# The RWKV inverse of a two-layer diffusion block: its broadcast load and its store laid out 32 by 4 instead of 4 by 32

## The chip, the core and the metric

The kernel runs on one core of a Trainium2 chip. A core has a matrix engine (TensorE, PE in the rows, with its weight loads as PEld), three engines for elementwise work (VectorE DVE, ScalarE ACT, GpSimd POOL), a queue engine that issues transfers (SyncE, SP) and 16 DMA engines that carry them out. Each engine works through its own list of instructions in order, and waits on semaphores for what others write. The metric is the device time of one execution in microseconds (us), lower is better; the figure compared is the median over runs.

## What is computed

Two layers over 512 latent tokens (x) and 256 context tokens (z) of width 1024. Each layer normalises, multiplies by one wide input projection, and feeds three token mixers: gated linear attention, windowed attention and a bidirectional RWKV-7 mixer. The mixers' outputs are merged, projected and added, and a gated feed-forward part follows. The RWKV mixer is, for each direction, a recurrence over tokens:

```
def step(S, inp):
    w_t, k_t, v_t, kk_t, a_t = inp[:5]
    sa = jnp.einsum('bhvk,bhk->bhv', S, kk_t)
    S = S * w_t[:, :, None, :] - sa[..., None] * (kk_t * a_t)[:, :, None, :] + v_t[..., None] * k_t[:, :, None, :]
    return S, jnp.einsum('bhvk,bhk->bhv', S, inp[5])
```

## The kernel before

The recurrence is done in chunks of 32 tokens. Within a chunk the dependence of each token on the earlier ones is a unit triangular 32 by 32 matrix, and the chunk needs its inverse. Four chunks (128 tokens, a "half" in the code) and 8 heads make 32 such blocks, which `inverse` (from line 1508) inverts together. There are 12 halves a layer, 6 in each direction, so 24 calls in all. The forward ones ("f") do their arithmetic on VectorE, the backward ones ("b") on GpSimd.

One call goes through these steps. All of its transfers are issued from SP.

- `prep` (from line 1450) loads `cp`, `bk` and `kr` (lines 1459 to 1461) and makes the scores `X`.
- Line 1516 stores the two quadrants of `X` to a DRAM tile `d1` (two DMAs of 64 KB).
- Line 1518 loads `d1` back, blocks on partitions, four copies of each block: `L`, 128 partitions of 4 KB, 512 KB.
- Line 1521 loads a start value (four pieces of a unit matrix) into `G`, 128 KB. `G` and `L` have two buffers each, shared by both directions, so this load can start only when an earlier half's `G` has been stored.
- Lines 1532 and 1533 run 31 pairs of multiply (`ftmp`) and subtract on `G` and `L`.
- Line 1536 stores `G` to a second DRAM tile `d2`, 128 KB in runs of 128 bytes, and line 1538 loads it back as `TT`, turned so that the matrix engine can use it.

A block's four partitions share its 32 rows: each works on the rows of one residue mod 4. `chain` (from line 1541) then takes the chunks of a half one after the other: `yp` (product with the state), `ysb` (ACT), `up` (product with `TT`, line 1584), `uv` (copies by DVE and ACT, line 1593), `sp` (line 50), `sblk` (the new state, DVE). `run` moves two such lanes, forward and backward, in turn. `ahead` lets the front (`prep` and `inverse`) of a lane run one half ahead in layer 0 and two in layer 1.

Beside these lanes the matrix engine works on products that need no mixer (`px`, `pz`), whose weights come as `raw` (512 KB each, line 66) and are split into `wh` (ACT, line 71) and `wl` (DVE, line 72). `paced` ties these products to the lanes' progress.

The order on each engine, SP's included, is not the order of the code. The kernel is built with a scheduler that simulates it with its own estimates of durations and sets each engine's order from that. A change in the code therefore reorders instructions far from it. Transfers complete when all their pieces have landed; SP itself issues in order, so a transfer that waits for data holds back all those behind it. The names in the rows leave buffer numbers out: `d` is both DRAM tiles, so `L<-d` is the load of line 1518, `d<-G` the store of line 1536 and `TT<-d` the load of line 1538.

Of the kernel before, what the change touches and what calls it, by code (L numbers as in the profile page):

```python
# [9 lines left out]
F32 = mybir.dt.float32  # L10
# [10 lines left out]
KD = 8  # L21
# [3 lines left out]
FREE, PER = 150, 3.3  # see paced()  # L25
# [3 lines left out]
class Kern:  # L29
# [18 lines left out]
    # ---------------------------------------------------------------- helpers  # L48
# [8 lines left out]
    def after(self, i, j):  # L57
        """instruction i, not before j in their engine's program"""
        self.tc.add_manual_dep(i.ins, j.ins.name, mybir.DependencyInfo(mybir.DependencyClass.NoSync, mybir.DependencyReason.DATA), reason="order")
        return i  # L60

    def wunit(self, src, n):
        """the next weights, split: per 128 columns the high and the low parts"""
# [20 lines left out]
    def hop(self, i):  # L84
        """a product of a chain that others are paced by"""
        if self.hops is not None:
            self.hops.append(i)

    def paced(self, i, ps):
        """beside a chain: the first FREE products (of 512 columns) as they come, then at most PER more after each one of the chain,  # L90
        so that those of the chain never queue behind many others"""
        if self.hops is not None:
            if self.done >= FREE and self.hops:
                self.after(i, self.hops[min(int((self.done - FREE) / PER), len(self.hops) - 1)])
            self.done += ps.shape[-1] / 512

    def room(self, n):
        """whether n more products fit the pace"""
        return self.done + n <= FREE + PER * len(self.hops)
# [10 lines left out]
    def run_job(self, later=None):  # L110
        """the next queued job; what a job returns is its second half, left to the caller if `later` is a list"""
# [14 lines left out]
    def rsqrt(self, y, s, t):  # L126
        """y = s ** -0.5 (s, y, t: same-shape SBUF tiles)"""
# [7 lines left out]
    def rsqrt_v(self, y, s, t):  # L135
        """y = s ** -0.5 without table functions: a guess from the halved exponent, three Newton steps"""
# [9 lines left out]
    # ---------------------------------------------------------------- consts  # L146
# [32 lines left out]
    # ---------------------------------------------------------------- adaLN  # L179
    def ada(self, l, bank, R, rbufs):  # L180
        """generator: modulation vectors of layer l, one round per 2048 columns; bank(shape, name): a PSUM tile, R: pool of the weights"""
# [36 lines left out]
    # ---------------------------------------------------------------- norm  # L218
    def stats(self, xk, a, b, P, tags, S, y):
        """generator: y <- 1 / rms of the tokens a..b-1 (rows 32 j: j-th quarter); P, tags: PSUM pool and (tag, bufs) of its one-bank tiles;  # L220
        S: pool of temporaries"""
# [18 lines left out]
    def spread(self, y, n, P, tags, S):  # L240
        """the n values of y, over all partitions (PSUM)"""
# [9 lines left out]
    def norm(self, xk, a, b, P, tags, S, apply):  # L251
        """generator: rmsnorm of the tokens a..b-1; apply(k, r): emits what follows for the k-th feature tile, r: 1 / rms over all partitions"""
# [10 lines left out]
    # ---------------------------------------------------------------- mixer input  # L263
    def gemm_x(self, w):
        """one 128-column tile of the input projection of the x tokens, feature-major"""
# [15 lines left out]
    def new_h(self, Z=None):  # L281
        """tiles of the two parts of h; Z: pool of the z tokens, where they lie apart"""
# [3 lines left out]
    def h(self, j, k, a, b):  # L286
        """part j (high, low) of the tokens a..b-1 of h, k-th feature tile"""
        return self.hz[j][k][:, a - NX:b - NX] if self.hz and a >= NX else self.hs[j][k][:, a:b]

    def norm_mod(self, xk, a, b, A, sh, P, tags, S, y=None):  # L290
        """generator: h = rmsnorm(x) * g * (1 + scale) + shift of the tokens a..b-1, split into two float32r parts;
        y: the tokens' 1 / rms, where they are known"""
# [21 lines left out]
    # ---------------------------------------------------------------- layers  # L314
    @contextmanager
    def weights(self, name, bufs, side=None):
        """pool of the weight tiles of the jobs to come; raw ones of their own only at the outermost level"""
# [14 lines left out]
    def fill(self):  # L332
        """one queued job, if any"""
# [6 lines left out]
    def mixed(self, gen, steps, spread):  # L340
        """run the mixer `gen` (about `steps` steps) with the queued jobs spread over it"""
# [9 lines left out]
    def layer(self, l, X, xs):  # L351
# [76 lines left out]
        with self.pool(f"pf{l}", space=PSUM) as pg:  # L428
# [5 lines left out]
            # layer 1: paced by the chain; layer 0, where TensorE is the bound: evenly from the start  # L434
# [30 lines left out]
        # merge, output projection, feed-forward  # L465
# [30 lines left out]
    def branch_jobs(self, l, n):  # L496
        """gated output projections of the first two mixers, summed into accd"""
# [24 lines left out]
    # tokens in two groups: those whose third mixer output comes last (0..127, 384..511) and the others  # L522
# [8 lines left out]
    def branch_operand(self, l, late, raw):  # L531
        """the third mixer's output of one group of tokens, in two parts"""
# [6 lines left out]
    def branch_gemm(self, l, w, m, late, g):  # L539
        """g <- gated product of one group of tokens"""  # L540
# [6 lines left out]
    def last_branch(self, l, n, P):  # L547
        """the third mixer's projection of the first group, added to what accd holds: the first group's operand of the output projection"""
# [18 lines left out]
    def gemm_parts(self, w, nk, rh, rl, parts):  # L567
        """products of the tokens of each part: (PSUM, first token, end)"""
# [51 lines left out]
    def two_parts(self, xs, parts, update, norm, keep=6):  # L620
        """the last KD queued jobs for the first part of the tokens, then for the second, with the first part's norm beside them;
        returns the second part's norm, not yet finished"""
# [25 lines left out]
    def ffn(self, l, n, xs):  # L648
# [3 lines left out]
        with self.ps, self.pool(f"fA{l}") as A:  # L652
# [27 lines left out]
            # the last update in two parts of the tokens, each part's norm as soon as it is there  # L680
# [19 lines left out]
            # the first tiles while the second part's norm is finished  # L700
# [22 lines left out]
    def final(self, xs, a, b, N, S):  # L723
        """generator: the final norm of the tokens a..b-1"""
# [30 lines left out]
# ------------------------------------------------------------------ gated linear attention  # L755
class Gla:
    """one layer's bidirectional gated linear attention; chunks of 128 tokens: x 0..3, z 4..5"""
# [77 lines left out]
    def cum(self, hp):  # L835
        """per-chunk cumulative log gates (times 16) of both directions for head pair hp"""
# [21 lines left out]
    def states(self, hp, B):  # L858
        """scaled queries, and the state before every chunk, of both directions"""
# [164 lines left out]
# ------------------------------------------------------------------ windowed attention  # L1024
class Swa:
    """one layer's grouped-query attention; tile t holds heads t and t + 4, key-value head g the rows 64 g"""

    def __init__(self, K, l, P, ps, yb):
# [13 lines left out]
        # float32r parts: a head's queries as (high; low) in one order of the row halves, keys twice  # L1042
# [5 lines left out]
    def add_jobs(self, P):  # L1048
        """projection jobs; P: pool of what only they need"""
# [46 lines left out]
    def run(self, T):  # L1096
# [4 lines left out]
        # the softmax of one group of heads beside the value products of the group before  # L1101
# [13 lines left out]
    def values(self, T, n, g, keys, r):  # L1115
        """generator: transposes of the weights, value products of one group of heads; its output when both groups are there"""
# [99 lines left out]
# ------------------------------------------------------------------ RWKV-7  # L1216
class Rwkv:
    """one layer's RWKV-7 mixer; tokens: x 0..511, z 512..767; halves of 128 tokens: x 0..3, z 4..5"""
# [9 lines left out]
    def open_f(self):  # L1228
        """what the projection jobs need"""
# [15 lines left out]
        self.hb = P.tile([128, 16], F32, name="hb")  # half of w0 (f p0..3, b p0..3), a0  # L1245
# [43 lines left out]
    # -- evacuation of a projected tile with the centred shift mix  # L1289
# [10 lines left out]
    def add_jobs(self, J, ps, psn):  # L1300
        """projection jobs; J: pool of temporaries, ps/psn: PSUM pool and (tag, bufs) of its one-bank tiles"""
# [14 lines left out]
        def lowrank(half, di, p, t):  # L1316
            """tanh of half the low-rank product plus half the offset"""
# [36 lines left out]
        def keys(p):  # L1354
            """normalised keys, and the two directions' replacement vectors and keys, of head pair p"""
# [67 lines left out]
    def knorm(self, J, bank, big, kt):  # L1423
        """1 / max(|k * k_k|, 1e-12) per head: rows 32 (token block) + head, columns x 0..127, z 128..191"""
# [23 lines left out]
    # -- decays and scores of 128 tokens of one direction  # L1448
    def prep(self, d, g):
# [31 lines left out]
        # transposed scores, rows (even chunk: B~ j, k~ j; odd chunk: k~ j, B~ j), columns (K~ i, r~ i)  # L1481
# [26 lines left out]
    def inverse(self, d, g):  # L1508
        """T = (I + L)^-1 of 32 blocks (4 chunks x 8 heads), four partitions per block (row mod 4)"""
        nc, T = self.nc, self.T  # L1510
        d1 = self.D.tile([2, 16, 32, 32], F32, name="d1", tag="d1", bufs=3)   # q, (e w p), j, i
        d2 = self.D.tile([8, 4, 32, 32], F32, name="d2", tag="d2", bufs=3)    # (q e w), p, j, i
# [5 lines left out]
        nc.sync.dma_start(L.rearrange("u j i -> u (j i)"), d1.rearrange("q u j i -> (q u) (j i)").unsqueeze(0).to_broadcast([4, 32, 1024]))  # L1518
# [17 lines left out]
        nc.sync.dma_start(d2.rearrange("m p (a s) i -> s (m p) a i", s=4), G)  # L1536
# [4 lines left out]
    def chain(self, it):  # L1541
        """generator: the chunks of one half of one direction"""
# [73 lines left out]
    def tail(self, g, y):  # L1616
        """group norm, bonus and gate of 128 tokens -> yc; rows of y: 32 (head pair) + token, columns: chunk, head, value"""
# [44 lines left out]
    def run(self):  # L1662
        """generator over the mixer's steps; yields "fill" where other work may be emitted"""
# [119 lines left out]
def _layout(x, c, ctx, c_ctx, w_ada, b_ada, g_mix, g_ffn, w_in, w_gk2, b_gk, g_gla, sink, mu_shift, w0, w_w2, a0, w_a2,  # L1783
            w_g2, k_k, k_a, r_k, gn_w, gn_b, w_branch, w_out, w_ffn1, w_ffn3, w_ffn2, g_final):
    f = np.float32
    D = {}
# [74 lines left out]
```

## Time and profile before

| what | value |
|---|---|
| time, three runs | 3356.23, 3366.86 and 3367.24 us, median 3366.86 |
| span of the profiled execution | 3361.6 us |
| PE busy over the span | 3033.8 us (90%) |
| DVE, ACT, POOL busy | 1756.6, 1081.2 and 990.4 us (52%, 32%, 29%) |
| mean granted clock of TensorE | 0.921 |
| DMA engines, the main queue | 34.2% of 16 engines' span |
| `L<-d`, `d<-G`, `TT<-d`, `G<-gid` | 24 each |

The span is the time from the first to the last instruction of one profiled execution. The profile gives no other time for that execution, so what lies around the span isn't shown; the median of the runs is 5.3 us above it. The granted clock is the share of full speed that TensorE was allowed: 1.00 is its upper level (2.4 GHz), 0.50 its lower one (1.2 GHz). The mixer's inverses lie in two stretches, about 645 to 1100 us (layer 0) and 2390 to 2870 us (layer 1).

### The profile page before, as it was taken

Reading aid. Unit: us, or ns where it says so; the run is one execution under the profiler, and the core shown is the slowest. Engines: PE = TensorE matmul, PEld = TensorE weight load, DVE = VectorE, ACT = ScalarE, POOL = GpSimd, SP = SyncE. Lnnn points to the kernel's source line nnn. Section 1 sums busy time; section 2 is a strip of 40 time slices with the busy share of each in tenths; the row PEclk is TensorE's granted clock in tenths of the full one; section 3 lists DMA queues with packets and bytes.
Section 4 is the critical chain, followed back from the end, with each engine's and each line's share of the span. In section 5 each row is a group of like instructions: output and inputs, shape, how many; then the busy total and the mean of one; then the engine's idle time right before and its main releaser. Section 6 shows DMA issues by size and latency. Waiting matters only on the chain. (4 is left out here: it accounts for less than half of the span.)

```text
span 3361.6 us, 62705 instructions
## 1 busy us (share of the span) xinstructions
PE 3033.8 (90%) x25760; PEld 2400.0 (71%) x25760; DVE 1756.6 (52%) x3506; ACT 1081.2 (32%) x2034; POOL 990.4 (29%) x1438
## 2 busy tenths in 40 slices
PE   6999999878889989999999899698857789799998
PEld 3777877666666778888888787576635466788887
DVE  3175557766656755222223454656567566643335
ACT  3255444422222233212122344453322222332223
POOL 2033122344655322101001211312266465221102
PEclk9999999888888999999999899798868679899999
DMA  7421222544345552443212322123633444512223
GB/s 289 153 74 56 96 101 95 174 131 124 99 119 142 168 197 73 153 157 132 63 63 95 96 73 95 58 76 126 205 103 107 112 131 137 187 69 95 96 98 119
DMA packets 269375, 398.33 MB, mean 118 GB/s; under 512 B 94624, under 2 KB 179360, under 8 KB 269088
## 3 DMA queue, kind: packets, MB, share of 16 engines
q1 hardware_dynamic: 249184, 370.20, 34.2%
q10 hardware_dynamic: 19904, 24.12, 2.0%
q8 instruction: 202, 3.31, 0.4%
q14 instruction: 85, 0.70, 0.1%
HBM read 320.33 MB, written 73.92 MB: 117 GB/s over the span
## 5 line engine op out<-in xcount | busy, mean ns | idle before, releaser
L50 PE MATMUL px<-hh,wl 128*128 128x512 f32 x1584 | 646.5, 408 | 31.9 <-DVE wl L72 31.8
L50 PE MATMUL px<-hh,wh 128*128 128x512 f32 x1584 | 651.9, 412 | 14.1 <-ACT wh L71 6.5
L50 PE MATMUL px<-hl,wh 128*128 128x512 f32 x1584 | 643.2, 406 | 11.6 <-POOL hl L302 8.8
L72 DVE TENSOR_TENSOR wl<-raw,wh 128x1024 fp32r<-128x1024 f32 (+1 forms) x314 | 402.3, 1282 | 366.4 <-ACT wh L71 332.1
L71 ACT ACTIVATE wh<-raw 128x1024 fp32r<-128x1024 f32 (+1 forms) x314 | 326.1, 1041 | 778.8 <-PE pz L50 395.2
L50 PEld LDWEIGHTS px<-hh,wl 128*128 128x128 f32 x1584 | 308.2, 195 | 110.0 <-DVE wl L72 38.1
L50 PEld LDWEIGHTS px<-hh,wh 128*128 128x128 f32 x1584 | 309.4, 195 | 106.7 <-issue 24.4
L50 PEld LDWEIGHTS px<-hl,wh 128*128 128x128 f32 x1584 | 308.8, 195 | 82.3 <-POOL hl L302 13.2
L673 POOL TENSOR_TENSOR al<-fs,ah 128x768 fp32r<-128x768 f32 (+1 forms) x44 | 85.0, 1931 | 726.3 <-ACT ah L672 726.3
L50 PE MATMUL pz<-hl,wh 128*128 128x256 f32 x872 | 253.1, 291 | 3.8 <-DVE hl L304 2.0
L50 PE MATMUL pz<-hh,wh 128*128 128x256 f32 x872 | 253.5, 292 | 1.5 <-DVE fs L663 1.4
L50 PE MATMUL pz<-hh,wl 128*128 128x256 f32 x872 | 252.0, 289 | 1.3 <-DVE wl L72 0.8
L50 PEld LDWEIGHTS pz<-hl,wh 128*128 128x128 f32 x872 | 171.2, 196 | 10.4 <-POOL hl L302 2.6
L50 PEld LDWEIGHTS pz<-hh,wh 128*128 128x128 f32 x872 | 170.3, 196 | 11.2 <-issue 3.2
L50 PE MATMUL px<-y,wh 128*128 128x512 f32 (+1 forms) x512 | 155.8, 391 | 24.8 <-ACT y L123 10.0
L50 PEld LDWEIGHTS pz<-hh,wl 128*128 128x128 f32 x872 | 170.4, 195 | 7.0 <-issue 5.2
L1532 POOL TENSOR_TENSOR ftmp<-G,L 128x60 f32<-128x60 f32 (+24 forms) x372 | 125.9, 338 | 146.9 <-DMA G<-gid 55.8
L1532 DVE TENSOR_TENSOR ftmp<-G,L 128x60 f32<-128x60 f32 (+24 forms) x372 | 107.4, 289 | 103.8 <-DMA G<-gid 55.6
L1533 POOL TENSOR_TENSOR G<-G,ftmp 128x60 f32<-128x60 f32 (+24 forms) x372 | 131.4, 353 | 25.2
L50 PE MATMUL sp<-uv,bkt 64*64 64x64 f32 x1536 | 99.8, 249 | 36.9 <-DVE uv L1593 36.5
L50 PEld LDWEIGHTS px<-y,wh 128*128 128x128 f32 x512 | 96.1, 209 | 44.2 <-ACT y L123 12.5
L50 PEld LDWEIGHTS sp<-uv,bkt 64*64 64x64 f32 x1536 | 69.3, 147 | 75.4 <-DVE uv L1593 41.1
(443 smaller groups left out, 6090.9 us busy)
## 6 DMA issues: line engine op xcount, KB each, us to landing
raw<-win SPq DMA_DIRECT2D x114, 512.0 KB
raw<-w SPq DMA_DIRECT2D x104, 512.0 KB
araw<-wada SPq DMA_DIRECT2D x96, 512.0 KB
raw<-w SPq DMA_DIRECT2D x48, 448.0 KB
kr<-krd SPq DMA_DIRECT2D x24, 512.0 KB
L<-d SPq DMA_DIRECT2D x24, 512.0 KB
gs<-gat ACTq DMA_DIRECT2D x24, 384.0 KB
raw<-wab SPq DMA_DIRECT2D x16, 512.0 KB
```

The source lines that it names most:

```text
L50: return self.nc.tensor.matmul(out, lhsT=lhsT, rhs=rhs, start=start, stop=stop)
L71: nc.scalar.activation(h[:, :n], raw[:, :n], AF.Copy)
L72: nc.vector.tensor_tensor(out=lo[:, :n], in0=raw[:, :n], in1=h[:, :n].bitcast(F32), op=ALU.subtract)
L673: nc.gpsimd.tensor_tensor(out=al, in0=s, in1=ah.bitcast(F32), op=ALU.subtract)
L1532: eng.tensor_tensor(out=t, in0=G[:, rows, j:j + 1].to_broadcast([128, a, m]), in1=L[:, j:j + 1, cols].to_broadcast([128, a, m]), op=ALU.mult)
L1533: eng.tensor_tensor(out=G[:, rows, cols], in0=G[:, rows, cols], in1=t, op=ALU.subtract)
```

## The change

The load keeps its bytes, but the four copies of a block now lie on neighbouring partitions: partition 4 u + s holds copy s of block u, where it was 32 s + u. The access pattern of its source in DRAM was 4 copies of 32 blocks of 1024 numbers; it is 32 blocks of 4 copies now. The start value in `gid` is rearranged in the same way, by the host's layout of constants. The store of `G`, one DMA whose outermost dimension was the four residues, becomes four DMAs, one for each residue, each from every fourth partition (32 partitions, 32 KB). The arithmetic on `G` and `L` has the same shapes. The rest of the diff removes comments.

```
@@ inverse @@
-        nc.sync.dma_start(L.rearrange("u j i -> u (j i)"), d1.rearrange("q u j i -> (q u) (j i)").unsqueeze(0).to_broadcast([4, 32, 1024]))
+        nc.sync.dma_start(L.rearrange("u j i -> u (j i)"), d1.rearrange("q u j i -> (q u) (j i)").unsqueeze(1).to_broadcast([32, 4, 1024]))
...
-        nc.sync.dma_start(d2.rearrange("m p (a s) i -> s (m p) a i", s=4), G)
+        for s in range(4):
+            nc.sync.dma_start(d2.rearrange("m p (a s) i -> s (m p) a i", s=4)[s], G[s::4])
@@ _consts @@
-            g[32 * s_:32 * s_ + 32, a, 4 * a + s_] = 1
+            g[s_::4, a, 4 * a + s_] = 1
```

Lines behind the store move down by one (`TT<-d` from 1538 to 1539, `uv` from 1593 to 1594). The scheduler's order is the same as before up to the first stores of layer 0, and differs on every engine from there on. Three places follow.

SP's queue around the first store of layer 0, before the change (the number behind `d` is that of the DRAM tile):

```order
L1518 DMA L<-d_7148 128x1x1024
L1536 DMA d_6578<-G 4x256x32
L1460 DMA bk<-bkdf_3850 128x4x256
L66 DMA raw<-win 128x1024
L1460 DMA bk<-bkdb_3851 128x4x256
L1538 DMA TT<-d_6578 128x8x32
```

The same place with the change:

```order
L1518 DMA L<-d_7154 128x1x1024
L1537 DMA d_6578<-G 256x1x32 x4
L66 DMA raw<-win 128x1024
L1460 DMA bk<-bkdf_3850 128x4x256
L1460 DMA bk<-bkdb_3851 128x4x256
L1539 DMA TT<-d_6578 128x8x32
```

The store's four DMAs stand together in the place of the one, and one weight load has moved ahead of a `bk` load.

SP's queue around the first stores of layer 1, before:

```order
L1518 DMA L<-d_23455 128x1x1024
L1536 DMA d_23172<-G 4x256x32
L1518 DMA L<-d_23461 128x1x1024
L1536 DMA d_23178<-G 4x256x32
L1538 DMA TT<-d_23172 128x8x32
L1521 DMA G<-gid 128x256
```

And with the change:

```order
L1518 DMA L<-d_23497 128x1x1024
L1537 DMA d_23208<-G 256x1x32 x4
L1537 DMA d_23214<-G 256x1x32 x2
L1539 DMA TT<-d_23208 128x8x32
L1537 DMA d_23214<-G 256x1x32 x2
L1518 DMA L<-d_23503 128x1x1024
L1521 DMA G<-gid 128x256
```

The first `TT` load now stands ahead of the second `L` load, and in the middle of the second store's four DMAs.

VectorE's list at the start of the third forward inverse of layer 0, before:

```order
L1606 TENSOR_TENSOR sblkb<-sp,scb 64x4x64 x2
L1532 TENSOR_TENSOR ftmp<-G,L 128x31
L1533 TENSOR_TENSOR G<-G,ftmp 128x31
L1593 COPY uv<-up 32x128
L1532 TENSOR_TENSOR ftmp<-G,L 128x30
L1533 TENSOR_TENSOR G<-G,ftmp 128x30
L1593 COPY uv<-up 32x128
```

And with the change:

```order
L1533 TENSOR_TENSOR G<-G,ftmp 128x8
L1594 COPY uv<-up 32x128 x2
L72 TENSOR_TENSOR wl<-raw,wh 128x1024
L1594 COPY uv<-up 32x128
L1532 TENSOR_TENSOR ftmp<-G,L 128x31
L1533 TENSOR_TENSOR G<-G,ftmp 128x31
```

Three of the copies `uv`, for which the matrix engine waits, and one weight split have moved ahead of the inverse's first multiply, which waits for `L` and `G`.

## Rows read from the trace of the kernel before

**Rows 1.** The page's head: span and number of instructions.

```profile
span 3361.6 us, 62705 instructions
```

**Rows 2.** Windows of the two stretches: length, engines' busy time, PEclk, DMA share, GB/s.

```profile
645.00:1100.00 455.00, 391.02 (x5140) 291.32 (x5136) 278.99 (x709) 117.80 (x280) 236.79 (x519) 0.86 0.46 132
2390.00:2870.00 480.00, 386.31 (x4962) 263.16 (x4960) 294.47 (x741) 118.46 (x283) 256.82 (x536) 0.78 0.45 129
```

**Rows 3.** PE's waits, 640 to 1200 us: total us, times, longest us.

```profile
PE sp L50 <- DVE uv L1593: 31.6, 7, 8.7
PE px L50 <- DVE wl L72: 11.6, 9, 6.7
PE xp L50 <- DVE bk L1477: 10.0, 2, 5.6
...
PE up L1584 <- DMA TT<-d: 3.7, 2, 2.1
```

**Rows 4.** PE's waits, 2400 to 2950 us.

```profile
PE up L1584 <- DMA TT<-d: 27.4, 4, 16.2
PE px L50 <- DVE wl L72: 19.0, 7, 10.8
PE xp L50 <- POOL kr L1479: 11.9, 2, 7.3
...
PE xp L50 <- DVE bk L1477: 9.1, 2, 7.2
```

**Rows 5.** Waits of the whole run: the inverse's first multiply, DVE and POOL.

```profile
POOL ftmp L1532 <- DMA G<-gid: 55.8, 6, 19.5
DVE ftmp L1532 <- DMA G<-gid: 55.6, 5, 21.0
...
POOL ftmp L1532 <- DMA L<-d: 34.5, 3, 16.6
DVE ftmp L1532 <- DMA L<-d: 33.0, 5, 9.3
```

**Rows 6.** Timeline of SP, 860 to 861 us: start, length, what.

```profile
860.40 0.57 SPq L1518 DMA_DIRECT2D L<-d  x1
```

**Rows 7.** Timeline of DVE from 872 us; in brackets the idle time before.

```profile
872.04 0.19 DVE L1532 TENSOR_TENSOR ftmp<-G,L 128x31 f32<-128x31 f32 x1 [9.32 <-DMA L<-d]
```

**Rows 8.** The chain that ended last, 2350 to 2950 us: start, length, what.

```profile
2429.57 12.69 DMA bk<-bkdf
...
2489.84 11.71 DMA d<-G
...
2634.39 2.41 DMA TT<-d
...
2675.36 4.92 DMA d<-G
...
2898.32 7.09 DMA raw<-wbc
...
2913.51 3.58 DMA raw<-wout
```

**Rows 9.** Windows; the last three: PEclk, DMA share, GB/s.

```profile
1032.60:1035.00 2.40, 2.40 (x19) 1.84 (x18) 0.69 (x1) 0.00 (x0) 0.00 (x0) 1.00 0.96 314
...
2494.00:2498.00 4.00, 0.00 (x0) 0.00 (x0) 0.00 (x0) 0.00 (x0) 0.00 (x0) 0.50 0.26 81
```

**Rows 10.** Timeline of SP, 2420 to 2520 us.

```profile
2482.65 7.11 SPq L1518 DMA_DIRECT2D L<-d  x1
...
2491.65 7.94 SPq L1538 DMA_DIRECT2D TT<-d  x1
```

**Rows 11.** Timelines of DVE and then PE about 2502 us.

```profile
2502.33 0.19 DVE L1532 TENSOR_TENSOR ftmp<-G,L 128x31 f32<-128x31 f32 x1 [21.02 <-DMA G<-gid]
...
2501.95 0.65 PE L1584 MATMUL up<-ysb,TT 32*32 32x64 f32 x16 [16.24 <-DMA TT<-d]
```

**Rows 12.** Timeline of PE about 785 us.

```profile
784.78 1.12 PE L50 MATMUL sp<-uv,bkt 64*64 64x64 f32 x12 [7.23 <-DVE uv L1593]
```

## Prediction

> **What bounds the kernel now.** The page gives the span, 3361.6 us [rows 1], and TensorE is by far the busiest engine, so a gain must come from where it isn't busy. I looked first at the windows of the two stretches that hold the inverses. In layer 0 TensorE works 391 of 455 us at a mean granted clock of 0.86, in layer 1 386 of 480 us at 0.78 [rows 2]. It thus stands idle for 64 and 94 us, 158 in all, and the lowered clock gives away (1 - 0.86) x 455 + (1 - 0.78) x 480 = 169 us of full speed.
>
> Then the matrix engine's list of waits in both stretches. The big entries are waits for the copies `uv`, the weight part `wl`, the scaled keys `bk` and `kr`, and for `TT` itself: 31.6 + 11.6 + 10.0 + 3.7 = 57 us [rows 3] and 27.4 + 19.0 + 11.9 + 9.1 = 67 us [rows 4], 124 us together. Only the last kind names one of the transfers that the change touches. The other kinds are ended by DVE or POOL, so the next question is what these stood still for: in the whole run the inverse's first multiply waited 56 us on each of the two engines for the start value `G` and 33 to 35 us on each for `L` [rows 5]. What is queued behind that multiply (`uv`, `wl`, the `kr` product) is what TensorE waits for. An example is the 7.2 us before `sp` at 784.8 us [rows 12], which stood behind a multiply that waited for `G`.
>
> Last, the transfers. An `L` load issued at 860.4 us was used at 872.0 us, 11.6 us later, and VectorE had been idle for 9.3 us [rows 6, 7]. Other loads of 512 KB landed in 3.6 and 7.1 us, and a `bk` load issued just behind two `L` loads took 12.7 us. The store `d<-G` took 11.7 us where an `L` load was ahead of it and 4.9 us on its own. The `TT` load, with the same bytes in the same runs of 128 bytes, took 2.4 us [rows 8]. The windows say why. With other loads in flight the DMA engines are busy at a share of 0.96. In a stretch with just an `L` load and a store in flight it is 0.26, about 4 of 16 engines, and everything else stands still at half clock [rows 9]. Both transfers have an outermost dimension of 4. They sit on the same quarter of the engines, so the store goes behind the load, and a third transfer is not even taken: SP was held for 7.1 us in issuing an `L` load and for 7.9 us in issuing `TT` [rows 10]. That one pile-up cost VectorE 21.0 us and TensorE 16.2 us [rows 11].
>
> **The change, part by part.** *Load.* With 32 outermost I expect all 16 engines, and so the time of other loads of the size: 3.6 us, at worst 7.1 [rows 8]. Against the 11.6 us shown this saves 4.5 to 8.0 us. I take 8.0, the time of the faster of two weight loads with the same 4 KB rows, and keep the other for the range.
>
> *Store.* One DMA becomes four. An issue takes SP about 0.57 us [rows 6], so the last piece is issued 1.7 us after the first. If it then lands as the whole `TT` load does, the store is done 1.7 + 2.4 = 4.1 us after its first issue; if it takes as long as the whole store did alone, 1.7 + 4.9 = 6.6 us [rows 8]. Behind an `L` load the saving is 11.7 - 4.1 = 7.6 us (5.1 at worst); alone it is 0.8 us (a loss of 1.7 at worst). I take the short end, as a piece is a quarter of the bytes.
>
> *What stood behind them.* Loads of `bk`, `kr`, `cp`, `G` and weights lose the queue in front of them: the 12.7 us of `bk` should fall towards 4, and the two holds of 7 to 8 us on SP [rows 8, 10] should go.
>
> *Three more issues per call.* 24 calls x 3 x 0.57 = 41 us more of SP's time. Behind the four issues stand weight loads and `TT`. SP mostly waits, so most of it is hidden. The path pays it where a late store was the wait, which is counted in the 4.1. I charge 3 us for weight loads that come late; without cover it would be the 41.
>
> *Arithmetic.* The products on `G` and `L` have the same shapes and count, so nothing changes there. The changed start value costs nothing at run time.
>
> *Order.* The lists change on every engine from the first stores on. The three places shown are neutral or good: the `uv` copies stand ahead of the waiting multiply, and `TT` ahead of an `L` load. I give the order no price, and keep it in the range.
>
> *Sum.* Of the 124 us I count as hit: the waits that name `TT` and the two on `bk` in layer 0, whole (27.4 + 3.7 + 10.0 = 41 us); of the other kinds the longest wait of each, which I could follow back to `L`, the store or a load behind them (8.7 + 6.7 + 10.8 + 7.3 + 7.2 = 41 us); and half of the remaining 42, 21 us [rows 3, 4]. That is 103 us. Each such wait should shrink by 7 to 8 us, which covers most of them whole. But the lists are in order, and behind a wait that goes the next one appears, mostly the serial pairs of `ftmp` and `G` on DVE and POOL. I let two thirds come back, 69 us; the ends are one third and all of it (34 and 103).
>
> The clock comes on top. Of the 169 us, a part lies in the idle time itself and costs nothing: if half of the 158 us falls at the low level, 0.5 x 79 = 39 us. Some 130 us then burden the work. If they fell with the idle time (69 of 158), 57 us would come back; but the stalls that stay keep the clock down too, so I take 24 us, between 0 and 57. The sum is 69 + 24 - 3 = 90 us: 3361.6 - 90 = 3271.6 us for that execution. With the 5.3 us by which the runs' median lies above its span I forecast **3277 us**.
>
> A rule speaks against the split store. In the Trainium skill's page "DMA: Bandwidth & Descriptors", section "Rules for kernel authors", small transfers should be merged into large ones, because under 64 KB one pays mostly overhead; each piece here has 32 KB. The trace bears out that small transfers are mostly overhead: the 128 KB of `TT` take 2.4 us, less than a weight load of four times the bytes, but not a quarter of it [rows 8]. If each piece paid these 2.4 us in turn, the store would take 9.6 us and save 2.1 instead of 7.6, and with half of the counted waits resting on the store about 25 us of the gain would go: 3302 us. I don't take this, as the start-up of several transfers in flight should overlap.
>
> That page's section "Why a DMA increments its semaphore by 16 and not by 1" says that a transfer runs on as many engines, up to 16, as divide the slowest dimension of both its sides. By it a 4 gives 4 engines, with which the share of 0.26 agrees, and the 32 would give 16; no run so far shows that, and the sum goes by the other loads alone.
>
> **The rivals.** *The waits are mostly replaced.* The inverse is a serial string of 62 instructions, and the lanes go one chunk at a time. If only a quarter or less of the 103 us comes back and none of the clock, the time is about 3367 - 25 = 3342 us. For it: two of the five long waits are reached through DVE or POOL work as well as a transfer. Against it: in the pile-up all engines stood still at once [rows 9, 11].
>
> *The lanes follow the transfers fully.* A lane has 6 calls a layer, one after the other. If each is shorter by 8.0 us for the load and 6 for the store (7.6 behind a load, 0.8 alone), 14 us, and the lanes set the length of both stretches, that is 6 x 14 x 2 = 168 us: 3199 us. Against it: the fronts run one or two halves ahead, so many calls have room.
>
> *Slower: the pieces don't overlap.* If each takes the 4.9 us of the whole store [rows 8] in turn, a store lasts 4 x 4.9 = 19.7 us, 8 us longer than in the pile-up and 15 longer than alone. `TT`, the next `G` and all that SP holds behind them come that much later. With ten of the 24 stores on the path at 8 us, less the 40 us that the faster `L` loads bring, the kernel is 40 us slower: 3407 us. It decides from 11.7 / 4 = 2.9 us a piece on; `TT`'s 2.4 us for all the bytes speaks against it.
>
> *The change doesn't do what it says.* If 32 outermost still runs on a quarter of the engines, nothing moves but the issues: about 3370 us.
>
> **How the numbers follow.** Forecast (a gain of 50 to 140 us): 0.66. Waits replaced (0 to 50 us): 0.19. Lanes follow fully (over 140 us): 0.07. Pieces in turn: 0.05. No effect: 0.03. The range is 3205 to 3350 us: its low end stands near the full lane gain, its high end at a gain of 17 us. It leaves out about 0.05 below and 0.14 above. Half a per cent, 17 us, is about what a measurement of this kernel can tell from no change. Faster by more takes the 0.66, the 0.07 and two thirds of the 0.19: 0.86. Within it: the rest of the 0.19 and the case of no effect, 0.09. Slower: 0.05.
>
> **What would show it.** In the changed profile the windows should show a DMA share well over 0.26 while `L` is in flight. First multiplies should wait for `L` and `G` a third as long as in [rows 5], the store in the chain should be 4 to 5 us, and no issue should hold SP for 7 us. PE's waits for `TT` should fall below 10 us, and both clocks should rise, to about 0.89 and 0.83. The forecast is wrong if the transfers shorten as said but the same PE time is lost to `uv` and `wl` behind DVE's own work, if `TT` comes later than before its four pieces, or if the new order puts other waits ahead of the `px` products.

## The result, and the profile after

The changed kernel takes 3259.47 us (median of four runs, 3251.93 to 3264.14) against 3367.05 us for the kernel before beside it (3356.23 to 3372.02). The ratio is 0.9685, 95% interval 0.9664 to 0.9706. The forecast was 3277 us, range 3205 to 3350. The page of the profiled execution after, its head and its first part:

```profile
span 3254.8 us, 62770 instructions
...
PE 2998.4 (92%) x25760; PEld 2383.2 (73%) x25760; DVE 1770.0 (54%) x3506; ACT 1081.6 (33%) x2034; POOL 997.9 (31%) x1438
```

The span fell by 3361.6 - 3254.8 = 106.8 us [rows 1]. TensorE's busy time fell by 3033.8 - 2998.4 = 35.4 us for the same number of instructions, so that part is clock. The remaining 71.4 us were idle time.

Where it went is read from SP's timeline: the first store of a block's scores (`d<-X`) and the last load of a result (`TT<-d`) bound the inverses of a layer. Before:

```profile
667.17 0.87 SPq L1516 DMA_DIRECT2D d<-X  x2
...
1089.53 0.37 SPq L1538 DMA_DIRECT2D TT<-d  x1
...
2415.88 1.70 SPq L1516 DMA_DIRECT2D d<-X  x2
...
2795.32 0.37 SPq L1538 DMA_DIRECT2D TT<-d  x1
```

After:

```profile
665.62 0.87 SPq L1516 DMA_DIRECT2D d<-X  x2
...
1048.08 0.38 SPq L1539 DMA_DIRECT2D TT<-d  x1
...
2370.49 2.06 SPq L1516 DMA_DIRECT2D d<-X  x2
...
2683.22 0.37 SPq L1539 DMA_DIRECT2D TT<-d  x1
```

Layer 0's stretch went from 422.4 to 382.5 us and layer 1's from 379.4 to 312.7 us, 39.9 + 66.7 = 106.6 us. The whole gain lies in the two stretches.

The windows after that answer to [rows 2] (length, busy time of PE, PEld, DVE, ACT, POOL, then PEclk, DMA share, GB/s):

```profile
645.00:1100.00 455.00, 423.01 (x5729) 319.43 (x5727) 318.13 (x772) 127.18 (x306) 263.28 (x538) 0.91 0.49 146
2320.00:2770.00 450.00, 388.40 (x5096) 269.40 (x5095) 322.62 (x809) 132.79 (x315) 267.01 (x545) 0.83 0.51 150
```

The clock is 0.91 where it was 0.86, and 0.83 where it was 0.78. These windows hold more work after than before, so idle time is better compared between the bounds above, where TensorE's counts of instructions differ by 2%. Before:

```profile
667.17:1089.53 422.36, 359.98 (x4798) 267.08 (x4797) 256.13 (x671) 108.16 (x262) 226.45 (x509) 0.85 0.45 125
2415.88:2795.32 379.44, 290.46 (x3686) 199.54 (x3685) 230.23 (x608) 90.24 (x210) 222.28 (x498) 0.76 0.44 123
```

After:

```profile
665.62:1048.08 382.46, 353.19 (x4871) 265.42 (x4873) 268.97 (x678) 108.46 (x263) 235.86 (x511) 0.89 0.48 142
2370.49:2683.22 312.73, 270.05 (x3613) 187.35 (x3611) 231.77 (x604) 88.60 (x205) 223.43 (x498) 0.81 0.52 147
```

TensorE idles 29 us in layer 0 where it was 62, and 43 us in layer 1 where it was 89.

Two short windows in which only an `L` load moves data, before and then after, show on how many DMA engines it runs:

```profile
1044.10:1046.10 2.00, 2.00 (x20) 1.06 (x20) 1.97 (x3) 0.00 (x0) 2.00 (x2) 0.50 0.25 63
```

```profile
929.50:930.60 1.10, 1.10 (x56) 0.93 (x50) 0.84 (x2) 0.27 (x1) 0.56 (x1) 1.00 0.99 380
```

A share of 0.25 of the 16 engines is 4 of them, and 0.99 is all 16.

The DMA issues after (KB each, median us from issue to landing), and the chain that ended last, which answers to [rows 8]:

```profile
L<-d SPq DMA_DIRECT2D x24, 512.0 KB, 4.6
...
G<-gid SPq DMA_DIRECT2D x24, 128.0 KB, 3.8
...
d<-G SPq DMA_DIRECT2D x96, 32.0 KB, 2.8
```

```profile
2382.31 4.91 DMA L<-d
...
2436.23 5.75 DMA bk<-bkdf
...
2485.75 3.59 DMA d<-G
```

An `L` load lands in 4.6 us where [rows 6, 7] showed 11.6 from issue to use, and `bk` in 5.8 where it took 12.7. The 3.6 us of `d<-G` are those of a store's last piece alone. Its first was issued earlier, as SP's timeline shows:

```profile
2483.87 2.49 SPq L1537 DMA_DIRECT2D d<-G  x4
```

The whole store thus took 2485.75 + 3.59 - 2483.87 = 5.5 us, where one took 11.7 behind a load. Of the 13 stores for which the trace has all four landings, the median from the first issue to the last landing is 4.4 us (3.9 to 5.7).

The waits of the inverse's first multiplies answer to [rows 5]; this view puts DVE's and POOL's together (us, times). SP's list of waits follows:

```profile
  DMA G<-gid: 33.5, 8
  DMA L<-d: 19.1, 5
```

```profile
SPq L1539 <- DMA d<-G: 14.9, 19, 2.5
```

The 111.4 us for `G` and 67.5 us for `L` of before have shrunk to 52.6 us together. The last line is SP standing at the issue of `TT` until the store has landed. In the kernel before, the same line read 75.8 us in 20 waits, the longest 11.5. As all these loads are issued by SP in order, whatever follows `TT` stood still as long.

SP was also held in issuing. In the kernel before, a transfer close behind an `L` load and a store often took 7 us or more to issue, as here:

```profile
815.20 0.57 SPq L1518 DMA_DIRECT2D L<-d  x1
815.86 0.59 SPq L1536 DMA_DIRECT2D d<-G  x1
816.55 9.56 SPq L1460 DMA_DIRECT2D bk<-bkdf  x1
```

There are nine issues of 7.1 to 9.8 us in that trace, 78.7 us together, all close behind an `L` load and a store; [rows 10] show two of them. After the change SP's longest issue takes 2.5 us. All issues of more than 1.5 us add up to 101.2 us before and 8.8 us after.

TensorE's own waits, in 640 to 1200 us and then in 2300 to 2900 us, answer to [rows 3, 4]:

```profile
PE px L50 <- DVE wl L72: 10.1, 10, 3.5
...
PE sp L50 <- DVE uv L1594: 4.3, 3, 3.4
...
PE xp L50 <- DVE bk L1477: 2.6, 1, 2.6
```

```profile
PE sp L50 <- DVE uv L1594: 9.9, 13, 2.4
...
PE px L50 <- DVE wl L72: 5.5, 7, 2.0
PE xp L50 <- POOL kr L1479: 4.6, 1, 4.6
PE up L1585 <- DMA TT<-d: 3.9, 2, 2.8
...
PE xp L50 <- DVE bk L1477: 2.0, 1, 2.0
```

The waits named in the prediction added up to 124 us. Of the same kinds 17 us are left in layer 0, with none for `TT`, and 16 us in layer 1, 33 together. (Layer 1's `uv`, which the 124 leave out, went from 4.9 to 9.9 us.) The longest single one was 16.2 us and is now 4.6. Other waits grew: that of `px` for `wh`, which ACT writes, went from 0.2 to 8.2 us in the first window.

### The profile page after: what moved, and what is told of

It is laid out like the page before. It is cut to its first block, busy times and chain, and to the rows that moved or that the text cites. A ratio compares the mean times of both kernels' runs of the same rounds, so it can differ in the third digit from the quotient of the medians.

```text
span 3254.8 us, 62770 instructions
## 1 busy us (share of the span) xinstructions
PE 2998.4 (92%) x25760; PEld 2383.2 (73%) x25760; DVE 1770.0 (54%) x3506; ACT 1081.6 (33%) x2034; POOL 997.9 (31%) x1438
## 5 line engine op out<-in xcount | busy, mean ns | idle before, releaser
L1532 DVE TENSOR_TENSOR ftmp<-G,L 128x60 f32<-128x60 f32 (+24 forms) x372 | 114.8, 309 | 23.0 <-DMA G<-gid 7.1
L231 POOL TENSOR_TENSOR sqa<-sqa,sq 128x256 f32<-128x256 f32 (+1 forms) x70 | 70.4, 1006 | 162.1 <-ACT sq L229 150.1
L1533 DVE TENSOR_TENSOR G<-G,ftmp 128x60 f32<-128x60 f32 (+24 forms) x372 | 112.6, 303 | 10.0
```

What stands on the lines that cost most here:

```text
L231: nc.gpsimd.tensor_tensor(out=acc[:, :n], in0=acc[:, :n], in1=sq[:, :n], op=ALU.add)
L1532: eng.tensor_tensor(out=t, in0=G[:, rows, j:j + 1].to_broadcast([128, a, m]), in1=L[:, j:j + 1, cols].to_broadcast([128, a, m]), op=ALU.mult)
L1533: eng.tensor_tensor(out=G[:, rows, cols], in0=G[:, rows, cols], in1=t, op=ALU.subtract)
```

## Experiments

"Wide" is a transfer with 32 outermost, "narrow" one with 4. In the kernels called pinned every engine is held to a recorded order of instructions by ordering constraints that wait for nothing, so that a kernel differs from another in its transfers and not in the scheduler's choices. The table has all of them; the last three columns are waits of the profiled execution: the first multiplies' for `G` and for `L`, and SP's at `TT` for the store.

| kernel | time, us | ratio to before, 95% | for `G` | for `L` | SP, store |
|---|---|---|---|---|---|
| before | 3367.05 | 1 | 111.4 | 67.5 | 75.8 |
| order_after_narrow | 3364.29 | 1.0006 (0.9989 to 1.0022) | 123.7 | 70.7 | 69.9 |
| narrow_load | 3351.34 | 0.9965 (0.9947 to 0.9982) | 89.9 | 77.8 | 49.8 |
| hold | 3348.03 | 0.9959 (0.9944 to 0.9974) | 106.3 | 24.1 | 10.2 |
| delay | 3328.71 | 0.9917 (0.9887 to 0.9946) | 78.1 | 49.2 | 14.9 |
| bystander | 3324.23 | 0.9897 (0.9869 to 0.9925) | 94.8 | 26.9 | 43.7 |
| eight_pieces | 3287.25 | 0.9782 (0.9759 to 0.9805) | 59.7 | 21.9 | 9.2 |
| narrow_store | 3275.05 | 0.9739 (0.9725 to 0.9754) | 17.9 | 28.9 | 42.0 |
| start_value_on_chip | 3271.26 | 0.9724 (0.9702 to 0.9747) | none | 60.8 | 27.6 |
| second_queue | 3270.18 | 0.9722 (0.9701 to 0.9743) | 30.8 | 17.5 | 46.6 |
| both_on_chip_and_queue | 3264.13 | 0.9708 (0.9690 to 0.9725) | none | 63.7 | 36.0 |
| changed kernel | 3259.47 | 0.9685 (0.9664 to 0.9706) | 33.5 | 19.1 | 14.9 |
| order_before_wide | 3257.86 | 0.9694 (0.9671 to 0.9716) | 34.6 | 15.5 | 22.3 |
| start_value_ahead | 3251.55 | 0.9672 (0.9642 to 0.9701) | none | 48.9 | 24.4 |

The kernel before was timed anew beside each group of runs: 3361.47 us for the order and the narrow ones, 3360.72 for bystander, delay, eight_pieces and start_value_ahead, 3364.11 for the other four. Ratios, not times, compare across groups.

**Order or transfers.** Two theories: the time came from the transfers, or from the new order that the scheduler chose for them. order_before_wide has the change's transfers in the order of the kernel before; order_after_narrow has the transfers of before in the changed kernel's order (its text without the added `pin_order` is the kernel before).

```
@@ kernel @@
         Kern(ctx, tc, I, out).emit()
+        pin_order(tc, nc)
```

> The change's transfers (load and store on 32 outermost), with every engine held to the order that the scheduler gave to the kernel before. If the gain comes from the transfers (theory), 3255 to 3300 us. If it comes from the new order (rival), about 3367 us.

> The transfers of before (load and store with 4 outermost), every engine held to the order of the changed kernel; a store stands where the last of the four stood. Theory: all of the gain goes, 3340 to 3400 us. Rival (the order): about 3260 us.

The order alone is worth nothing that can be told from zero (1.0006), and the transfers in the old order give the whole gain (0.9694).

**Load or store.** Both are pinned to the changed kernel's order. narrow_load has the load of before and four wide stores, narrow_store four wide loads and the store of before, both in the old layout of partitions:

```
@@ narrow_load, against the kernel before @@
-        nc.sync.dma_start(d2.rearrange("m p (a s) i -> s (m p) a i", s=4), G)
+        for s in range(4):
+            nc.sync.dma_start(d2.rearrange("m p (a s) i -> s (m p) a i", s=4)[s], G[32 * s:32 * s + 32])
@@ narrow_store, against the kernel before @@
-        nc.sync.dma_start(L.rearrange("u j i -> u (j i)"), d1.rearrange("q u j i -> (q u) (j i)").unsqueeze(0).to_broadcast([4, 32, 1024]))
+        for s in range(4):
+            nc.sync.dma_start(L[32 * s:32 * s + 32].rearrange("u j i -> u (j i)"), d1.rearrange("q u j i -> (q u) (j i)"))
```

> Order of the changed kernel, four wide stores, but the load with 4 outermost in the old layout. Theory: the load is the larger part, since it also stands in front of the store and of the loads behind it: 3330 to 3370 us. Rival (the store is the larger part): below 3300 us.

> Order of the changed kernel, the load as four wide DMAs in the old layout, but the store as one DMA with 4 outermost. Theory: with nothing slow in front of it the store takes about 5 us as it did alone, so little is lost: 3260 to 3285 us. Rival (the store is the larger part): above 3310 us.

The load is worth 3364.29 - 3275.05 = 89 us. The store is worth 3364.29 - 3351.34 = 13 us, and 0.9739 - 0.9685 = 0.0054, some 18 us, once the load is wide. The 89 and the 13 us are net of the 72 issues that each of these edits adds. The 18 us are not: narrow_store has as many issues as the changed kernel, as its load comes in four. One wide load with one narrow store was not run, so what the four stores bring beside it, issues paid, is not shown. The first multiplies' and SP's waits of narrow_load:

```profile
  DMA G<-gid: 89.9, 9
  DMA L<-d: 77.8, 9
```

```profile
SPq L1539 <- DMA d<-G: 49.8, 22, 6.5
```

With a narrow load and wide stores the wait for `L` is no shorter than before. But the wait for `G`, whose load is the same in both, grows as much over the changed kernel's (by 56 us, that for `L` by 59). A narrow load delays more than itself.

**The inverse's own wait, or what queues behind it.** Theory one: the gain is that of the inverse, which gets its `L` sooner. Theory two: it is that of the loads behind the narrow transfer. bystander keeps the wide `L` load and puts a narrow copy of the same 512 KB behind it, which nobody reads. delay makes `L` itself late, by two copies of the blocks ahead of it, with nothing narrow. hold has such copies behind `L`, three in a chain, so that `L` is on time and SP stands still all the same. All three are pinned to the changed kernel's order.

```
@@ bystander, behind the load of L @@
+        dx = self.D.tile([4, 32, 1056], F32, name="dx", tag="dx", bufs=3)
+        nc.sync.dma_start(dx[:, :, 0:1024], d1.rearrange("q u j i -> (q u) (j i)").unsqueeze(0).to_broadcast([4, 32, 1024]))
@@ delay, ahead of the load of L, which then reads src in place of d1; hold, behind it, with range(3) and 9 buffers @@
+        src = d1
+        for _ in range(2):
+            dn = self.D.tile([2, 16, 32, 32], F32, name="dn", tag="dn", bufs=6)
+            nc.sync.dma_start(dn.rearrange("q u j i -> (q u) (j i)"), src.rearrange("q u j i -> (q u) (j i)"))
+            src = dn
```

> The changed kernel in its order, plus, right behind each L load, a copy of the same 512 KB from DRAM to a DRAM tile that nobody reads, with 4 outermost. The L load keeps its 16 engines, so what the inverse waits for is short, but a quarter of the engines is held as before. If the queue in front of other transfers is what the narrow load cost (theory), most of the 89 us comes back: 3320 to 3360 us. If the cost was the inverse's own wait for L (rival), 3260 to 3290 us.

> The changed kernel in its order, but the blocks are first copied twice from DRAM to DRAM (128 KB, all 16 engines), each copy waiting for the one before; then the L load reads the second copy. L comes about 5 us later, no engine is crowded, and SP stands still while the copies land. If the inverse's own wait for L is the cost (rival), most of the 89 us comes back: 3330 us or more. If it is the queue in front of others (theory), 3265 to 3300 us.

> The changed kernel in its own order on every engine, with three more copies of the 128 KB of blocks from DRAM to DRAM behind each load of L, the second waiting for the first and the third for the second. So SP stands still for two landings in every call and issues three more DMAs, as in the run delay, but L itself is not late. In delay the time rose by 69 us over the changed kernel. Theory that the inverse's own wait for a late L is what costs there: here only the issues are left, 72 at 0.3 us as in eight_pieces, 22 us, so 3265 to 3290 us. Rival, that what costs is SP standing still, with the loads of weights, keys and start values queued behind it: as slow as delay, 3310 to 3340 us. Between the two, both share it in that proportion.

bystander is 65 us slower than the changed kernel by the medians (0.0212 of the ratio, some 71 us), though `L` is waited for 26.9 us and not 67. delay came out 69 us slower, well over the theory's range and just short of the rival's. Its profile shows why that was no clean test: SP waits 65.6 + 44.8 = 110 us for the copies. hold was made for that, and is slower still, by 89 us, above both of its ranges. Its profile, first the first multiplies' waits, then SP's:

```profile
  DMA G<-gid: 106.3, 9
  DMA L<-d: 24.1, 5
```

```profile
SPq L1522 <- DMA dn<-d: 86.5, 24, 5.7
...
SPq L1522 <- DMA dn<-dn: 45.0, 24, 2.4
```

One such place on SP's timeline, and the first multiply on DVE that waited for it:

```profile
2466.03 0.54 SPq L1518 DMA_DIRECT2D L<-d  x1
2466.63 0.59 SPq L1522 DMA_DIRECT2D dn<-d  x1
2470.09 2.89 SPq L1522 DMA_DIRECT2D dn<-dn  x2
...
2479.14 0.61 SPq L1518 DMA_DIRECT2D L<-d  x1
2479.80 0.60 SPq L1522 DMA_DIRECT2D dn<-d  x1
2483.40 2.83 SPq L1522 DMA_DIRECT2D dn<-dn  x2
2486.28 0.58 SPq L1526 DMA_DIRECT2D G<-gid  x1
```

```profile
2488.93 0.19 DVE L1537 TENSOR_TENSOR ftmp<-G,L 128x31 f32<-128x31 f32 x1 [7.40 <-DMA G<-gid]
```

With 4.3 us to land (the median there), both `L` loads were in by 2483.4. `G` was issued only at 2486.28, right behind the copies that held SP, and used 2.65 us later. The DMA view gives `G` loads even a shorter median to land here than in the changed kernel (3.0 us against 3.8), while the wait for them is three times as long. It is a wait for the issue, not for the transfer.

SP stood 131.5 us in hold and 110.4 us in delay for the copies, and the time rose by 89 and 69 us. Part of that is not standing still: hold has three more issues a call and delay two (not three, as the expectation of hold says), 72 and 48 in all. At the 0.3 us an issue that the next part finds, these are 22 and 14 us, and 67 and 55 us are left, 0.5 us for each us that SP stood. As both come to the same, delay needs no cost of its own for a late `L`. That the inverse's own wait would show as the main cost fell.

**What an issue costs.** eight_pieces is pinned and splits each store once more, second_queue gives half of the four pieces to ScalarE's queue.

```
@@ eight_pieces, inside the loop over s @@
-            nc.sync.dma_start(d2.rearrange("m p (a s) i -> s (m p) a i", s=4)[s], G[s::4])
+            for h in range(2):
+                nc.sync.dma_start(d2.rearrange("m p (a s) i -> s (m p) a i", s=4)[s, 16 * h:16 * h + 16], G[64 * h + s:64 * h + 64:4])
@@ second_queue, the same line @@
+            (nc.sync if s % 2 == 0 else nc.scalar).dma_start(d2.rearrange("m p (a s) i -> s (m p) a i", s=4)[s], G[s::4])
```

> The changed kernel in its order, each store as eight DMAs of 16 partitions. 24 x 4 more issues of 0.57 to 0.61 us are 55 to 59 us of SP. The prediction charged 3 us for the first 72 extra issues, so 3260 to 3270 us; if issues lie on the path (rival), 3280 us or more.

> The changed kernel, scheduled anew, with the second and fourth piece of each store issued by ScalarE instead of SP. SP then has 48 issues fewer. Theory from eight_pieces, that an added issue on SP costs about 0.3 us of the span: 3240 to 3250 us against 3259 for the changed kernel. Rival: ScalarE now waits for the end of each inverse in its own program, and the evictions and exponentials queued behind it come late; then it is slower than the changed kernel, 3265 to 3300 us. If SP's issues are all hidden and ScalarE has room: 3255 to 3263 us.

96 more issues cost 28 us (33 by the ratios), some 0.3 us each, although the pieces land sooner (1.9 us against 2.8) and SP waits less for the store (9.2 us against 14.9). The wait for `G` rose from 33.5 to 59.7 us. Taking 48 issues off SP gave nothing back, however: the ratio is not below that of the changed kernel. SP's list of waits in second_queue shows one reason:

```profile
SPq L1539 <- DMA d<-G: 46.6, 31, 4.7
```

SP stands at `TT` three times as long as in the changed kernel. ScalarE is not late with its pieces: its last issue of a store ends at most 0.5 us after SP's last, in all 24. But SP, with two issues fewer, is at `TT` sooner, and the pieces take longer to land than the 2.8 us of the changed kernel (median in the last column):

```profile
d<-G ACTq DMA_DIRECT2D x48, 32.0 KB, 3.3
d<-G SPq DMA_DIRECT2D x48, 32.0 KB, 3.4
```

Why they land later is not shown. So 0.3 us is the price of further issues, and no run shows that the change's own 72 cost as much.

**The wait that is left.** Three kernels, scheduled anew, take away the first multiply's wait for `G`: four buffers of `G` in layer 1, or a start value that is kept on chip and copied into `G` by the engine that runs the inverse, or this with second_queue.

```
@@ start_value_ahead @@
-        G = T.tile([128, 8, 32], F32, name="G", tag="G", bufs=2)
+        G = T.tile([128, 8, 32], F32, name="G", tag="G", bufs=2 if self.zout else 4)
@@ start_value_on_chip: gid is loaded once a layer, as bfloat16; ftmp has 80 columns instead of 128 @@
-        nc.sync.dma_start(G, self.I["gid"])
...
         eng = nc.vector if d == "f" else nc.gpsimd
+        eng.tensor_copy(G, self.gid)
```

> The changed kernel with four buffers for G instead of two in layer 1 (layer 0 has no room), in the scheduler's own order. The start value can then be loaded before the earlier store has landed. If the waits for G that are left (33.5 us on VectorE in eight, over both layers) are on the path, 3235 to 3255 us; if not, the same as the changed kernel within 10 us.

> The changed kernel, scheduled anew, but the start value of G is loaded once a layer and copied into G by the engine that runs the inverse (VectorE or GpSimd), in place of a DMA for each call. This takes away 24 issues of SP, 7 us at 0.3 us each, and the wait of the first multiply for G from DRAM. Theory that these waits still lie on the path: 3225 to 3250 us against 3259 for the changed kernel. Rival: the waits for G sit where the engine would wait for L anyway, or have room, and the two engines get 24 more copies: 3250 to 3265 us.

> The edits of second_queue and start_value_on_chip together, scheduled anew. SP has 72 issues fewer than the changed kernel, as many as the change added. If both gains hold and are independent: 3215 to 3240 us. If the issues are what counts and nothing else: 72 at 0.3 us, 3235 to 3245 us. Rival, that ScalarE's waits cost what SP's issues give back: 3250 us or more.

None is shown to be faster than the changed kernel; all intervals overlap with its own. start_value_on_chip lies above both of its ranges, both_on_chip_and_queue in its rival's, and the 3251.55 us of start_value_ahead fit either of its two. The wait changes its name. The first multiplies of start_value_on_chip and the copies ahead of them:

```profile
  DMA L<-d: 60.8, 12
```

```profile
  DMA d<-G: 29.3, 12
```

No multiply waits for `G` now, but those for `L` wait 60.8 us where it was 19.1, and the copies wait 29.3 us for the buffer that the store before must have left. That is 90 us where the changed kernel has 52.6.

## Why the prediction was right

**What bounds it.** Right. The gain lies in the two stretches, and is idle time and clock.

**Load.** The mechanism was right, the size 1 us off: 4.6 us to land (3.7 to 7.4) against the 3.6 taken, inside the 3.6 to 7.1 given. The Trainium skill's page "DMA: Bandwidth & Descriptors", section "Why a DMA increments its semaphore by 16 and not by 1", gives a transfer as many engines, up to 16, as divide its slowest dimensions: 4 for the 4 of before, 16 for the 32 here. The trace agrees: with `L` alone the share is 0.25 before and 0.99 after.

**Store.** By its own size right: 4.4 us in the median, against 4.1 forecast. But its worth was not. Weighing the rule on small transfers, the prediction let half of the counted waits rest on the store; the runs give it 13 to 18 us of the 107. Most of its 11.7 us of before came from the load ahead of it, and goes when that load is wide: SP's longest wait for the store was 11.5 us before and is 4.4 us in narrow_store.

**The rule on small transfers** (the Trainium skill's page "DMA: Bandwidth & Descriptors", section "Rules for kernel authors") did not decide here: the one store was narrow, and narrow_store, with as many issues in all, is the slower by 0.0054. Once the transfers are wide the rule points the right way, as eight_pieces shows.

**What stood behind them.** Right, and more important than the prediction made it. It named the loads behind the narrow transfer and two issues that held SP for 7 to 8 us. It did not name the other seven, nor the 75.8 us in which SP stood at `TT` for the store, which fell to 14.9. With the 92 us less of long issues, SP was freed of some 153 us. What these are worth can only be estimated. hold and delay put 0.5 us of time on each. In narrow_store SP stood 27 us longer at `TT` than in the changed kernel and 41 us longer in issues of more than 1.5 us, for 16 to 18 us of time, about 0.25 for each. That makes 38 to 77 of the 107 us, before the change's own 72 issues are paid. The rest I put down to the loads' own lateness, `L`'s among them, which is argued from bystander and not measured by itself: there SP stood 29 us longer at `TT` and 43 us longer in such issues, worth 18 to 36 us by the same prices, and the kernel lost 65 to 71. How much the lateness of `L` alone costs stays open, as no kernel here makes `L` late with nothing behind it touched. The 89 us of the load less bystander's 65 to 71 would leave 18 to 24 us, if the two add up.

**Issues.** Charged at 3 us. The runs don't measure the charge itself: at the price that further issues have in eight_pieces, 0.3 us, 72 would be about 22 us, and second_queue doesn't tell what they cost, as it moves a wait along with them. The expectation for eight_pieces was too low in the same way.

**Order.** No price, and shown to have none.

**Sum.** 69 us of idle time against 71.4 measured, and 24 us of clock against 35.4. The clock is the term that was too small; no run shows why. That the idle term fits so closely is in part luck. It was two thirds of 103 us of waits that should be hit. PE's waits of the kinds counted fell by 91 us, from 124 to 33, and its idle time by 71, as other waits grew: less was hit than forecast, and more of it came back than two thirds.

**The rivals.** That waits would mostly be replaced (3342 us) fell with the 71 us; that the lanes follow fully (3199 us) fell too, as the two layers gained 39.9 and 66.7 us where 84 each were given. Pieces in turn would have had `TT` later: PE's wait for it is 3.9 us in layer 1, not over 27, and a store takes 4.4 us, not 19.7. That the 32 would change nothing fell with the share of 0.99.

## What to carry to other kernels

A DMA with a small outermost dimension costs more than its own landing: price what its queue issues next, and what waits for those loads. Look in the issuing engine's list of waits for the place where it stands for a store before it may issue the load back; that line told more here than the list of the compute engines. Look on its timeline, too, for issues that take several microseconds, as they hold back everything queued behind them. When the wait for one of two inputs is taken away, look at once at the other, since both may come from the same queue.

## What had not been expected

The start value's load is not touched by the change, but the wait for it went from 111.4 to 33.5 us, a larger fall than that of `L` (67.5 to 19.1). Each of a store's four pieces of 32 KB lands in 2.8 us (median), each of eight of 16 KB in 1.9 us, and SP waits less for the eight; yet the kernel with eight is slower. And a late `L` needs no cost of its own to explain delay: with `L` on time, but SP standing still longer and three issues more a call, hold was slower than delay, and both lose 0.5 us for each us that SP stood.
